# Dealing the first half's indexer tiles among product pairs, gating state-space output in SBUF halves, and exponentiating decay rows that are already on chip

## The chip, the cores and the metric

The kernel runs on one core of a Trainium2 chip. TensorE (PE) multiplies matrices from SBUF into eight PSUM banks; VectorE (DVE), ScalarE (ACT) and GpSimd (POOL) do the elementwise work; every transfer between the chip's memory and SBUF is issued on the queue of SyncE (SP). Each engine works through its own list of instructions in order, and waits at an instruction until what it needs is there. The metric is the device time of one execution in microseconds (us).

## The reference

One layer of a streaming encoder over 1024 positions of width 2048. One input projection makes every part:

```python
u = jnp.einsum('bsd,de->bse', h, w_in[layer])
q, k, v, z_attn, q_idx, k_idx, w_idx, z_ssd, xbc, dt_raw = _split_cols(u, IN_WIDTHS)
o_attn = _dsa_attention(q, k, v, q_idx, k_idx, w_idx) * jax.nn.silu(z_attn)
o_ssd = _ssd_mixer(xbc, z_ssd, dt_raw, conv_w[layer], conv_b[layer], dt_bias[layer], a_log[layer], d_skip[layer], ssd_norm_w[layer])
sub = jnp.einsum('bse,ed->bsd', jnp.concatenate([o_attn, o_ssd], axis=-1), w_out[layer])
h = _layer_norm(DEEPNORM_ALPHA * h + sub, ln_g[layer], ln_b[layer])
```

The attention has an indexer: 16 small heads give scores `relu(q_idx . k_idx)`, summed with the weights `w_idx`; each query keeps its top 256 admissible keys (by chunks of 64) and attends to those. The state-space mixer (SSD) makes, per group of four heads, decay matrices out of cumulative sums `a_cum`, a part within a chunk and a part from the state carried over, which is scaled by `exp(a_cum)`. Its output y is gated: `g = y * silu(z)`, divided by the root of the mean square over the group, times `norm_w`. All of it is float32.

## The kernel before, in words

**Float32 on the array.** Each matrix operand is split into a high and a low part (`xh`, `xl` of the activations, `wh`, `wl` of the weights) and a product is three matmuls: xh by wh, xl by wh, xh by wl. The splits are made by ACT (the high part) and DVE (the low part).

**Who sets the order.** Every step of the computation is a generator, a task with a priority, that says before each step what it needs: engines, free buffers, events (`Need`). `Flow` (line 353) keeps a clock for each engine by a model; whenever PE has been given one piece of the main stream, `pump` (line 476) takes tasks that `ready` (line 431) lets through, and their instructions are written behind those already there. So the order on all engines is fixed when the kernel is built, and each engine's list is one interleaving of main stream and tasks. All instructions are recorded at one helper line, L312, so the trace is read by the names of buffers: `pj` are the four PSUM banks of projections and products, `a` the three of scores and small products, `o` one more; `u` the 29 general SBUF buffers of 128x512, `s` larger ones, `xr`, `xh`, `xl` activations, `wr`, `wh`, `wl` weights; names such as `mx`, `my`, `y`, `zs`, `arow`, `ts`, `c` are arrays in the chip's memory.

**The main stream.** `units` (line 589) makes it out of `PLAN` (line 55). The positions are in two halves, h=1 the second and h=0 the first. First come nine tiles for h=1: `misc` (the indexer's key, its weights, and dt) and eight tiles `qi` of 128 indexer columns, that is, two indexer heads each. Then the same nine for h=0, with the `qi` tiles on 256 columns only (`s0=256`), because the first 256 positions keep all admissible keys. Then two groups of pairs of tiles. The two halves of the positions and the two tiles of a pair make a 2x2 block product that is computed with fewer block products out of sums of blocks, in four phases (`product`, line 663); within a phase, pairs are taken in couples of two. Group 0 has eight pairs (four couples): k, v, the q heads and the first xbc columns. Group 1 has xbc, zs and z. Last come seven output products on sums of blocks of the mixed output (`PRODUCTS`, line 67: A11, S3, S1, S2, A22, S4, A12), numbered 0 to 6, each of eight banks of 24 matmuls, and the layer norm.

**A qi tile's tail.** When its 48 matmuls have filled a `pj` bank, `t_qi` (line 1452) applies the rope on DVE (a shuffle and three multiplies or adds), which also frees the bank for PE; then for each head and block of queries PE computes scores into an `a` bank, ACT applies the relu there, and DVE multiplies by the head's weight and adds to the sum in `s` (`t_score`, line 1494). `t_topk` (line 1518) then finds each query's threshold in 32 rounds between ACT and DVE.

**State-space part.** `t_ssd` (line 1928) is a task for each half h and group g, in two steps cp=0,1 of 256 positions. A step loads xy, B and C, loads the decay rows `ar` from `arow` (all 128 partitions get each head's row), and later loads the same rows again in another arrangement, `ea`, with four transfers, and exponentiates them. `ev_y` signals that both steps have been written to the array `y`. `t_gate` (line 2046) loads two tiles of y and (unless they are still in SBUF) two of silu(z), which `s_zs` (line 1909) saved in `zs`; it multiplies, squares, sums by PE, scales, and writes two of the sixteen arrays `mx` of a half. The forms of the output products (`t_form`, line 1011) read `mx` back: one load for A11, two with a difference for S3, three with two sums for S1 and S2.

## Time and profile before

| | |
|---|---|
| time, median of 3 runs | 1709.56 us (1708.21 to 1709.71) |
| the profiled execution's own time | 1706.55 us |
| its span, first to last instruction | 1704.4 us |
| mean granted TensorE clock | 0.982 |
| PE busy | 1631.9 us (96%), 7996 matmuls |
| DVE busy | 1328.9 us (78%) |
| ACT busy | 985.3 us (58%) |
| POOL busy | 174.2 us (10%) |
| moved by DMA | 426.55 MB |

By the trace the stages lie so, in us from the start of the span: tiles for h=1 to 125; tiles for h=0 to 254; phase 0 of group 0 to 358.5, its other phases to 622; group 1 to 1329.5; output product 0 from there to 1392, product 1 to 1451, product 2 to 1517, the other four to 1692; the rest of the layer norm to 1704.4.

How to read it: the busy time of PE is the time in which some matmul was under way, and a matmul under a throttled clock is busy for longer, so a busy PE can still lose time. The granted clock stands beside it. A row of the view by windows gives the window, its length, then busy time and number of instructions of PE, of the weight loads, of DVE, ACT and POOL, then the granted clock, the busy share of the DMA engines and GB/s. A row of a timeline gives start, duration, engine, operation, and in brackets the idle time before it with what ended it.

### The profile page before, as it was taken

How to read it: one execution, taken by the hardware profiler on the slowest of the kernel's cores; microseconds unless marked ns; L12 is line 12 of the kernel's file. 1: busy time of each engine (PE TensorE's matmuls, PEld its weight loads, DVE VectorE, ACT ScalarE, POOL GpSimd, SP SyncE). 2: the span in 40 equal slices, each digit the busy share in tenths (PEclk: the TensorE clock that was granted, in tenths of full speed). 3: DMA queues.
4: the chain of work that ended last, by engine and by line, in shares of the span. 5: the costliest groups of instructions: out<-in, count | busy, mean ns of one | idle time of the engine just before them, and what ended most of it. 6: DMA issues, size and time to landing. Idle time of an engine off the chain costs nothing.

```text
span 1704.4 us, 24034 instructions
## 1 busy us (share of the span) xinstructions
PE 1631.9 (96%) x7996; PEld 1347.0 (79%) x7996; DVE 1328.9 (78%) x2411; ACT 985.3 (58%) x1750; POOL 174.2 (10%) x198
## 2 busy tenths in 40 slices
PE   9998889989998999999999999999999989899997
PEld 7787667868876878888888888888888768688885
DVE  5799989688878976767787678976687675649998
ACT  4554567988887568847444446785746443432330
POOL 0000000000000000212011201211111000000110
PEclk9998999999999999999999999999999999899999
DMA  8297523699978877568785487667989889767754
GB/s 302 70 313 275 207 99 120 225 353 329 351 261 304 305 267 259 194 218 297 273 313 190 162 281 232 204 198 226 316 309 332 288 292 301 251 240 266 242 191 155
DMA packets 203876, 426.55 MB, mean 250 GB/s; under 512 B 21224, under 2 KB 61288, under 8 KB 203752
## 3 DMA queue, kind: packets, MB, share of 16 engines
q1 hardware_dynamic: 203320, 424.63, 72.4%
q8 instruction: 63, 1.03, 0.2%
q14 instruction: 61, 0.50, 0.1%
q10 hardware_dynamic: 432, 0.39, 0.1%
HBM read 317.06 MB, written 107.87 MB: 249 GB/s over the span
## 4 chain that ended last, share of the span: by engine, by line
PE 53%; DVE 19%; ACT 11%; DMA 10%; issue 5%; SPq 1%; POOL 1%; DVEq 0%; ACTq 0%
PE pj L312 39%; PE a L312 11%; DVE u L312 8%; ACT u L312 5%; DVE wl L312 3%; DVE s L312 3%; PE o L312 3%; ACT wh L312 2%; DVE wr L312 2%; DMA wr<-wt 2%; DVE xl L312 1%; SPq L312 1%; DMA s<-xt 1%; DMA u<-xt 1%; DMA u<-o 1%
## 5 line engine op out<-in xcount | busy, mean ns | idle before, releaser
L312 PE MATMUL pj<-xh,wh 128*128 128x512 f32 (+1 forms) x1496 | 587.8, 393 | 27.1 <-DVE u L312 20.1
L312 PE MATMUL pj<-xl,wh 128*128 128x512 f32 (+1 forms) x1496 | 574.0, 384 | 1.2 <-DVE xl L312 1.1
L312 PE MATMUL pj<-xh,wl 128*128 128x512 f32 (+1 forms) x1496 | 574.0, 384 | 0.5 <-DVE wl L312 0.5
L312 DVE TENSOR_TENSOR wl<-wr,wh 128x1024 fp32r<-128x1024 f32 (+2 forms) x232 | 278.0, 1202 | 183.8 <-ACT wh L312 176.9
L312 ACT ACTIVATE wh<-wr 128x1024 fp32r<-128x1024 f32 (+2 forms) x242 | 248.4, 1031 | 189.8 <-PE pj L312 153.6
L312 PEld LDWEIGHTS pj<-xh,wh 128*128 128x128 f32 x1496 | 284.9, 190 | 83.3 <-issue 24.6
L312 PEld LDWEIGHTS pj<-xh,wl 128*128 128x128 f32 x1496 | 284.5, 190 | 56.3 <-DVE wl L312 1.0
L312 PEld LDWEIGHTS pj<-xl,wh 128*128 128x128 f32 x1496 | 285.3, 191 | 52.0 <-DVE xl L312 2.2
L312 PE MATMUL a<-u,u 128*128 128x512 f32 (+3 forms) x736 | 173.7, 357 | 7.7 <-DVE s L312 4.1
L312 DVE TENSOR_TENSOR u<-u,u 128x512 f32<-128x512 f32 (+6 forms) x231 | 149.7, 660 | 10.5 <-DMA u<-o 4.2
L312 PEld LDWEIGHTS a<-u,u 128*128 128x128 f32 x736 | 121.2, 191 | 44.6 <-DVE s L312 21.2
L312 PE MATMUL pj<-wh,xh 128*128 128x512 f32 x310 | 126.7, 409 | 15.3 <-ACT xh L312 8.2
L312 ACT ACTIVATE u<-a 128x512 fp32r<-128x512 f32 (+4 forms) x112 | 53.4, 489 | 137.8 <-DVE u L312 58.5
L312 ACT ACTIVATE u<-s,sm 128x768 bf16<-128x768 int16 (+7 forms) x132 | 129.5, 981 | 1.5
L312 ACT ACTIVATE u<-u 128x512 f32<-128x512 f32 (+4 forms) x165 | 91.0, 563 | 63.8 <-DVE u L312 55.7
L312 PE MATMUL pj<-wh,xl 128*128 128x512 f32 x310 | 122.3, 395 | 2.3 <-DVE xl L312 2.3
L312 PE MATMUL pj<-wl,xh 128*128 128x512 f32 x310 | 122.3, 394 | 0.0
L312 ACT ACTIVATE a<-a 128x512 f32<-128x512 f32 (+3 forms) x160 | 76.2, 503 | 65.8 <-PE a L312 64.4
L312 DVE TENSOR_TENSOR wr<-wr,wr 128x1024 f32<-128x1024 f32 (+1 forms) x87 | 106.1, 1220 | 7.7 <-DMA wr<-wt 7.3
L312 DVE TENSOR_TENSOR u<-pj,u 128x512 f32<-128x512 f32 (+2 forms) x112 | 74.5, 667 | 25.8 <-PE pj L312 23.9
L312 POOL TENSOR_SCALAR s<-s,sm 128x640 f32<-128x640 f32 (+7 forms) x64 | 60.1, 953 | 245.9 <-DVE sm L312 188.6
L312 PEld LDWEIGHTS pj<-wh,xh 128*128 128x128 f32 x310 | 59.0, 190 | 30.7 <-ACT xh L312 9.1
(254 smaller groups left out, 2151.2 us busy)
## 6 DMA issues: line engine op xcount, KB each, us to landing
wr<-wt SPq DMA_DIRECT2D x187, 512.0 KB, 5.1
u<-u SPq DMA_DIRECT2D x110, 256.0 KB, 4.8
wr<-t SPq DMA_DIRECT2D x44, 512.0 KB, 8.5
u<-wo SPq DMA_DIRECT2D x64, 256.0 KB, 6.1
ts<-u SPq DMA_DIRECT2D x64, 256.0 KB, 4.2
wr<-ts SPq DMA_DIRECT2D x32, 512.0 KB, 4.6
u<-mx SPq DMA_DIRECT2D x54, 256.0 KB, 6.3
s<-xt SPq DMA_DIRECT2D x24, 512.0 KB, 7.8
```

Of the source, the lines that this page charges most:

```text
L312: f(*args, **kw)
```

## The change

Three edits.

1. **Tiles of the first half.** The line of `PLAN` for h=0 goes. Its nine tiles (written by the same `plain`) are dealt among the four couples of group 0, phase 0: misc, couple 0, couple 1, qi a to d, couple 2, qi e to h, couple 3. The tiles read the x blocks that phase 0 reads anyway.
2. **Gating.** The arrays `y`, `zs` and the upper eight of `mx` (now pairs, `my`) are laid out so that both 128-row tiles of a group are one transfer of 128x2x256, half the positions. When silu(z) has been saved by the end of a step of `t_ssd`, the step's output stays in SBUF and goes straight to a `t_gate` for that step; only zz, the half of silu(z), is loaded. Otherwise y is saved and loaded as before, in halves. `t_gate` handles 256 positions at a time, except where silu(z) itself is still in SBUF (`wide`).
3. **Decay exponentials.** `ea` is computed by ACT out of the rows `ar` that are on chip, 64 partitions at a time, before `ar` is overwritten; the four transfers, the wait for a buffer between, and the one exponential on all 128 partitions go. Its buffer is asked for at the start of a step (`u=8 - cp`).

```diff
 PLAN = [
     (1, FIRST + QI[2:], 3),
-    (0, [("misc", 0)] + QI, 3),
     [(("k", 0), ("k", 1)), (("v", 0), ("v", 1))] + [(("q", n), ("q", n + 4)) for n in range(4)]
     + [(("xbc", (0, 2 * j)), ("xbc", (0, 2 * j + 1))) for j in range(2)],
     [(("xbc", (1, j)), ("xbc", (3, j))) for j in range(4)] + [(("xbc", (2, j)), ("xbc", (2, 2 + j))) for j in range(2)]
     + [(("zs", (n // 2, n % 2)), ("z", n)) for n in range(8)],
 ]
 GROUPS = [x for x in PLAN if isinstance(x, list)]
+OPENING = "m01abcd2efgh3"
...
             for ph in range(4):
-                for couple in couples:
+                for couple in [int(k) if k.isdigit() else k for k in OPENING] if (gi, ph) == (0, 0) else couples:
+                    if isinstance(couple, str):
+                        tile = ("misc", 0) if couple == "m" else QI["abcdefgh".index(couple)]
+                        for u in range(2):
+                            plain(0, tile, u, base)
+                        continue
+                    couple = couples[couple] if isinstance(couple, int) else couple
                     for f in range(1 + (ph < 3)):
                         for c in couple:
                             i = put(self.product(gi, c, pairs[c], ph, f, base + 2 * ph + f))
...
-        self.mixed = [[self.scratch(f"mx{h}_{e}", [P, HALF]) for e in range(16)] for h in range(2)]
+        self.mixed2 = [[self.scratch(f"my{h}_{g}", [2, P, HALF]) for g in range(4)] for h in range(2)]
+        self.mixed = [[self.scratch(f"mx{h}_{e}", [P, HALF]) for e in range(8)] + [m[j] for m in self.mixed2[h] for j in range(2)]
...
-        if self.ev_y[h, g].t is None:
-            yield Need()
-            fl.dma(self.zs_sc[h, g, j], x)
+        yield Need()
+        other = self.zg.get((h, g, 1 - j))
+        if other[0] is None if other else len(self.ydone[h, g]) < 2:
+            fl.dma(self.zs_sc[h, g][j], x)
             fl.free(x)
             x = None
         fl.signal(e)
         self.zg[h, g, j] = (x, e)
-        if (h, g, 1 - j) in self.zg:
-            fl.add(self.t_gate(h, g), 2, f"gate{h}{g}")
+        if other:
+            if x is not None:
+                fl.add(self.t_gate(h, g, (0, 1)), 2, f"gate{h}{g}")
+            else:
+                for cp in self.ydone[h, g]:
+                    fl.add(self.t_gate(h, g, (cp,)), 2, f"gate{h}{g}")
+
...
-            yield Need("", s4=1, u=7 - cp, keep=SKEEP)
+            yield Need("", s4=1, u=8 - cp, keep=SKEEP)
...
-            bn, xdt, xdd, hs = [fl.new("u", [P, 2, 256]) for _ in range(4)]
+            bn, xdt, xdd, hs, ea = [fl.new("u", [P, 2, 256]) for _ in range(5)]
+            ea = ea.rearrange("p a (b l) -> p a b l", b=2)
             rows = self.arow[h].rearrange("(c n) l -> c n l", c=4)[2 * cp:2 * cp + 2, 4 * g:4 * g + 4, :]
-            pairs = rows.rearrange("c (j q) l -> q c j l", q=2)
             for k in range(2):
                 fl.dma(ar[:, k], rows[k].partition_broadcast(P))
...
+            for q in range(2):
+                rq = slice(64 * q, 64 * q + 64)
+                fl.act(ea[rq], ar[rq].rearrange("p k (j q) l -> p k j q l", q=2)[:, :, :, q], AF.Exp)
...
-            yield Need("", u=1)
-            ea = fl.new("u", [P, 2, 2, P])
-            for q in range(2):
-                for k in range(2):
-                    fl.dma(ea[64 * q:64 * q + 64, k], pairs[q, k].partition_broadcast(64))
             yield Need("A")
             fl.act(ar, ar, AF.Exp, scale=-1.0)
-            fl.act(ea, ea, AF.Exp)
             yield Need("VG")
...
+            zz, landed = None, 0.0
+            if self.zg_there(h, g) and fl.avail("us"):
+                zz = fl.new("us", [P, 2, 256])
+                fl.dma(zz, self.zs_sc[h, g][:, :, cp * 256:cp * 256 + 256].rearrange("j p s -> p j s"))
+                landed = fl.cells[-1][0]
...
+            if self.zg_there(h, g):
+                fl.add(self.t_gate(h, g, (cp,), xy, zz), 2, f"gate{h}{g}", max(fl.clk["V"], fl.clk["G"], landed))
+                continue
             yield Need()
-            fl.dma(self.y_sc[h, g][:, :, cp * 256:cp * 256 + 256], xy)
+            self.ydone[h, g].append(cp)
+            fl.dma(self.y_sc[h, g][:, :, cp * 256:cp * 256 + 256].rearrange("j p s -> p j s"), xy)
             fl.free(xy)
+            fl.signal(self.ev_y[h, g, cp])
+            if self.zg_there(h, g):
+                fl.add(self.t_gate(h, g, (cp,)), 2, f"gate{h}{g}")
         fl.free(hs)
-        fl.signal(self.ev_y[h, g])
...
-    def t_gate(self, h, g):
+
...
+        w = 256 * len(cps)
+        cols = slice(256 * cps[0], 256 * cps[0] + w)
+        held = [self.zg[h, g, j] for j in range(2)]
+        wide = held[0][0] is not None
+        evs = () if xy is not None else tuple(self.ev_y[h, g, cp] for cp in cps)
+        yield Need("", us=(xy is None) * (1 if w == 256 else 2) + (zz is None and not wide), ev=evs + tuple(e for _, e in held))
...
+            if zz is None:
+                zz = fl.new("us", [P, 2, 256])
+                fl.dma(zz, self.zs_sc[h, g][:, :, cols].rearrange("j p s -> p j s"))
+            if xy is None:
+                xy = fl.new("us", [P, 2, 256])
+                fl.dma(xy, self.y_sc[h, g][:, :, cols].rearrange("j p s -> p j s"))
+            xs, zs, tiles = [xy], [zz], [xy, zz]
+            part = lambda t, j: t[0][:, j]
...
+        n = self.gated[h, g] = self.gated.get((h, g), 0) + len(cps)
+        if wide:
+            for j in range(2):
+                fl.dma(self.mixed[h][8 + 2 * g + j], xs[j])
+        else:
+            fl.dma(self.mixed2[h][g][:, :, cols].rearrange("j p s -> p j s"), xy)
+        if n == 2:
+            for j in range(2):
+                fl.signal(self.ev_mix[h, 8 + 2 * g + j])
+        fl.free(*tiles)
```

In the order, PE's rows go from 7392 to 7405, DVE's from 2279 to 2294, POOL's from 184 to 188, and ACT's keep their number; single transfers on SP go from 1315 to 1235: 64 of `arow` fewer, 14 fewer writes and 14 fewer reads of `y`, and 6 more writes and 6 more reads of `z`, the gates of the attention, which are saved when they are ready ahead of the attention's output.

**First place: PE at the end of the h=0 misc tile**, where the second of the h=0 tiles' banks follows it. A matmul row names the bank, the activation part, the weight part and the shape. Before, the misc tile and the first qi tile (`pj_1544`) are interleaved and the next qi tile, `pj_1609`, follows:

```order
L312 MATMUL pj_1544<-xh_1364,wl_1407 128x256
L312 MATMUL pj_1544<-xh_1368,wh_1406 128x256
L312 MATMUL pj_1544<-xl_1369,wh_1406 128x256
L312 MATMUL pj_1544<-xh_1368,wl_1407 128x256
L312 MATMUL pj_1609<-xh_1240,wh_1486 128x256
L312 MATMUL pj_1609<-xl_1241,wh_1486 128x256
L312 MATMUL pj_1609<-xh_1240,wl_1487 128x256
L312 MATMUL pj_1609<-xh_1244,wh_1486 128x256
```

With the change, the first of the two products of couple 0, `pj_1578`, follows the misc tile (`pj_1474`):

```order
L312 MATMUL pj_1474<-xh_1462,wl_1391 128x512
L312 MATMUL pj_1474<-xh_1466,wh_1390 128x512
L312 MATMUL pj_1474<-xl_1467,wh_1390 128x512
L312 MATMUL pj_1474<-xh_1466,wl_1391 128x512
L312 MATMUL pj_1578<-xh_1224,wh_1470 128x512
L312 MATMUL pj_1578<-xl_1225,wh_1470 128x512
L312 MATMUL pj_1578<-xh_1224,wl_1471 128x512
L312 MATMUL pj_1578<-xh_1228,wh_1470 128x512
```

What moved: tiles of 256 columns with a tail of scores no longer follow each other; a product on 512 columns stands there, and qi a comes after four such products.

**Second place: DVE ahead of the rope that frees a bank.** Before, `pj_1609` above takes the bank of `pj_1151`, the last but one qi tile of h=1; its rope is the shuffle and the three operations on `pj_1151` and `u_1595`:

```order
L312 TENSOR_TENSOR wl_1539<-wr_1202,wh_1538 128x1024
L312 SCALAR_TENSOR_TENSOR s_109_761<-a_1551,wsc_244,s_109_761 128x384
L312 SCALAR_TENSOR_TENSOR s_110_762<-a_1565,wsc_244,s_110_762 128x512
L312 TENSOR_TENSOR s_271_1532<-s_270_1530,s_271_1532 128x1024
L312 TENSOR_TENSOR s_270_1530<-xr_1534,s_270_1530 128x1024
L312 TENSOR_TENSOR wl_1587<-wr_1274,wh_1586 128x1024
L312 TENSOR_TENSOR u_1113<-u_1113,u_1393 128x512
L312 TENSOR_TENSOR u_1111<-u_1111,u_1113 128x512
L312 STREAM_SHUFFLE u_1595<-pj_1151 128x512
L312 TENSOR_TENSOR pj_1151<-pj_1151,u_642 128x512
L312 TENSOR_TENSOR u_1595<-u_1595,u_643 128x512
L312 TENSOR_TENSOR u_1594<-pj_1151,u_1595 128x512
```

With the change the same tile is `pj_1135`, and its bank goes to `pj_1632`, the second product of couple 0:

```order
L312 TENSOR_TENSOR s_271_1516<-s_270_1514,s_271_1516 128x1024
L312 TENSOR_TENSOR s_270_1514<-xr_1518,s_270_1514 128x1024
L312 TENSOR_TENSOR u_1097<-u_1097,u_1377 128x512
L312 TENSOR_TENSOR u_1095<-u_1095,u_1097 128x512
L312 TENSOR_TENSOR u_1541<-u_1082,u_1541 128x512
L312 TENSOR_TENSOR wl_1575<-wr_1258,wh_1574 128x1024
L312 STREAM_SHUFFLE u_1586<-pj_1135 128x512
L312 TENSOR_TENSOR pj_1135<-pj_1135,u_626 128x512
L312 TENSOR_TENSOR u_1586<-u_1586,u_627 128x512
L312 TENSOR_TENSOR u_1585<-pj_1135,u_1586 128x512
```

What moved: DVE's list there is nearly the same, with one more small operation ahead of the rope; PE's list has changed ahead of the bank's next use, which now follows the first 24 matmuls of `pj_1578`.

**Third place: SP in output product 2** (before) and the same forms' loads with the change. Before, forms of S1 (`xh_14456`, `xl_14458`, `u_14460` and the three from `mx_7`, `mx_15`) stand among a y write, four decay transfers, silu loads and y loads of the last SSD step, whose gated result goes to `mx_14` and `mx_15`:

```order
L312 DMA xh_14456<-mx_6_261 128x512
L312 DMA xl_14458<-mx_14_269 128x512
L312 DMA u_14460<-mx_6_277 128x512
L312 DMA y_1_326<-xh_13949 256x1x256
L312 DMA u_14503<-mx_7_262 128x512
L312 DMA u_14505<-mx_15_270 128x512
L312 DMA u_14507<-mx_7_278 128x512
L312 DMA u_14516<-arow_292 64x2x128 x4
L312 DMA s_5_400<-u_14430 128x512
L312 DMA xh_14528<-zs_1_0_339 128x512
L312 DMA u_14530<-zs_1_1_340 128x512
L312 DMA u_14532<-y_1_326 128x512
```

With the change, the loads of the same two forms read `my_3` (with `mx_6`, `mx_7`); the rest is weights (`wr`), one half of silu(z), one write of a gated half (`my_3_262`, which is of the other half of the positions), and two writes of forms to `s_5` and `s_6`:

```order
L312 DMA u_14314<-mx_6_269 128x512
L312 DMA u_14316<-my_3_258 128x512
L312 DMA u_14318<-mx_6_277 128x512
L312 DMA my_3_262<-u_13500 128x2x256
L312 DMA u_14341<-zs_1_326 128x2x256
L312 DMA s_5_384<-u_14239 128x512
L312 DMA xl_14391<-mx_7_270 128x512
L312 DMA u_14393<-my_3_258 128x512
L312 DMA u_14395<-mx_7_278 128x512
L312 DMA wr_14415<-ts_01_356 128x1024
L312 DMA xl_14423<-zs_2_327 128x2x256
```

What moved: the decay transfers and the y transfers are gone from between the loads and what follows them.

More of the change, by code (lines that the diff above doesn't have):

```diff
@@ L1924, in s_zs, with zg_there @@
         self.zg[h, g, j] = (x, e)
-        if (h, g, 1 - j) in self.zg:
-            fl.add(self.t_gate(h, g), 2, f"gate{h}{g}")
+        if other:
[4 more added lines that the diff above has]
+                    fl.add(self.t_gate(h, g, (cp,)), 2, f"gate{h}{g}")
+    def zg_there(self, h, g):
+        return all((h, g, j) in self.zg for j in range(2)) and self.zg[h, g, 0][0] is None
     def t_ssd(self, h, g):
@@ L2058, in t_gate @@
         yield Need("G")
-        for j in range(2):
-            fl.two(xs[j], xs[j], zg[j], ALU.mult)
+        for x, z in zip(xs, zs):
+            fl.two(x, x, z, ALU.mult)
         yield Need("A")
-        for j in range(2):
-            fl.act(zg[j], xs[j], AF.Square)
+        for x, z in zip(xs, zs):
+            fl.act(z, x, AF.Square)
         yield Need("G")
-        fl.two(zg[0], zg[0], zg[1], ALU.add)
+        fl.two(part(zs, 0), part(zs, 0), part(zs, 1), ALU.add)
         yield Need("P", a=1, sm=1)
```

46 lines of the change are left out of this document (21 added, 25 removed).

## The prediction

> **What bounds the kernel now.** I read the page first, then the view by windows along the stages.
>
> ```profile
> PE 1631.9 (96%) x7996; PEld 1347.0 (79%) x7996; DVE 1328.9 (78%) x2411; ACT 985.3 (58%) x1750; POOL 174.2 (10%) x198
> ...
> PEclk9998999999999999999999999999999999899999
> ```
>
> ```profile
> 24.00:125.00 101.00, 98.64 (x455) 80.83 (x456) 81.19 (x140) 52.52 (x97) 6.00 (x5) 1.00 0.59 206
> 125.00:254.00 129.00, 110.23 (x604) 89.47 (x603) 120.80 (x192) 73.58 (x127) 6.52 (x5) 0.91 0.54 197
> 254.00:358.50 104.50, 103.72 (x464) 84.82 (x463) 81.62 (x193) 88.32 (x176) 8.61 (x14) 1.00 0.59 214
> 358.50:622.00 263.50, 248.81 (x1075) 202.29 (x1074) 217.69 (x449) 200.50 (x377) 9.80 (x13) 0.98 0.88 312
> 622.00:1329.50 707.50, 703.62 (x3693) 591.66 (x3692) 532.69 (x983) 429.94 (x753) 115.37 (x130) 1.00 0.74 249
> 1329.50:1517.00 187.50, 169.23 (x858) 138.83 (x857) 114.41 (x188) 81.05 (x144) 8.91 (x7) 0.95 0.79 266
> 1517.00:1704.40 187.40, 175.38 (x770) 143.68 (x768) 167.66 (x250) 45.42 (x55) 17.41 (x12) 0.98 0.67 227
> ```
>
> PE is the bound, but not evenly. In group 1 (622 to 1329.5) it is busy for 703.6 of 707.5 us at a full clock: nothing is to be had there. It is idle for 18.8 us in the first half's tiles (125 to 254), for 14.7 in the rest of group 0 and for 18.3 in output products 0 to 2, and in the first and the last of these the clock is low too. In 125 to 254 it is DVE that is full, 120.8 of 129, while on either side of it DVE has some 20 us to spare. The view of waits says who is waited for, over the span and then in 125 to 254:
>
> ```profile
> PE pj L312 <- DVE u L312: 27.1, 6, 7.6
> PE pj L312 <- ACT xh L312: 8.9, 4, 4.5
> ```
>
> ```profile
> PE pj L312 <- DVE u L312: 15.6, 4, 7.6
> ```
>
> **What a stall in the tiles looks like**, in the timelines of PE and of DVE:
>
> ```profile
> 131.82 0.28 PE L312 MATMUL pj<-xh,wh 128*128 128x256 f32 x1
> ...
> 142.88 0.55 PE L312 MATMUL pj<-xh,wh 128*128 128x256 f32 x1 [7.59 <-DVE u L312]
> 143.24 0.41 PE L312 MATMUL pj<-xl,wh 128*128 128x256 f32 x1
> 143.45 0.41 PE L312 MATMUL pj<-xh,wl 128*128 128x256 f32 x1
> ```
>
> ```profile
> 135.18 1.22 DVE L312 TENSOR_TENSOR s<-s,s 128x1024 f32<-128x1024 f32 x1
> ...
> 140.05 0.72 DVE L312 STREAM_SHUFFLE u<-pj 128x512 f32<-128x512 f32 x1
> ...
> 142.05 0.69 DVE L312 TENSOR_TENSOR u<-pj,u 128x512 f32<-128x512 f32 x1
> ```
>
> ```profile
> 135.00:143.00 8.00, 0.41 (x4) 0.23 (x2) 7.83 (x12) 1.28 (x2) 0.00 (x0) 0.67 0.76 258
> 143.00:150.00 7.00, 7.00 (x34) 6.69 (x35) 6.79 (x11) 2.29 (x5) 1.04 (x2) 0.65 0.99 322
> ```
>
> DVE works without a gap (7.83 of 8 us), the rope that frees the bank ends at 142.7, and PE starts then. Its next matmuls come 0.21 us apart instead of 0.12, at a clock of 0.65 for 7 us. So a stall costs its length and then some.
>
> **What is lost in 125 to 254.** The groups of PE in that window:
>
> ```profile
> L312 PE MATMUL a<-u,u 128*128 128x512 f32 x136 | 45.0, 445 | 3.1 <-DVE s L312 2.1
> L312 PE MATMUL pj<-xh,wh 128*128 128x256 f32 x128 | 39.3, 307 | 15.7 <-DVE u L312 15.6
> L312 PE MATMUL pj<-xl,wh 128*128 128x256 f32 x127 | 38.1, 300 | 0.0
> L312 PE MATMUL pj<-xh,wl 128*128 128x256 f32 x127 | 37.9, 299 | 0.0
> L312 PE MATMUL pj<-xh,wh 128*128 128x512 f32 x16 | 6.4, 401 | 0.0
> ```
>
> The durations overlap, so I go by pitch. Where PE runs without a gap and at full clock, four output products of 192 matmuls each take 175 us, 228 ns for one of 512 columns:
>
> ```profile
> 1517.00:1692.00 175.00, 174.82 (x769) 143.54 (x768) 159.19 (x236) 45.42 (x55) 16.43 (x11) 1.00 0.68 231
> ```
>
> One of 256 columns takes 119 (the rows at 131.7 to 131.9). 382 by 119 is 45.5; 136 and three times 16 by 228 is 41.9; the 38 smaller ones, by their widths, are 5.0. That is 92.4 us of work in 129: **36.6 are lost**, 18.8 idle and 17.8 in a slow clock.
>
> **Edit 1, the tiles dealt out.** PE's work stays the same; its 604 matmuls and the 464 of phase 0 are mixed. DVE's work for both stretches is one row:
>
> ```profile
> 125.00:358.50 233.50, 213.94 (x1065) 174.29 (x1064) 202.42 (x384) 161.91 (x303) 15.13 (x19) 0.95 0.57 204
> ```
>
> PE alone would need 233.5 − 36.6 = 197, DVE alone 202.4: the two are nearly equal, so DVE need not hold PE up for long anywhere, but it has next to nothing in hand. The least gain is where DVE keeps the share that it reached in the tiles (120.8 of 129, 0.936): 202.4/0.936 = 216, a gain of 17. The most is all 36.6. I take **−26**, half way: DVE is then at 202.4 of 207.5, as full as in the 8 us of its row at 135. The first stall shows how close it is: counted in the order with these pitches, PE has 8.0 us more work ahead of `pj_1632` than it had ahead of `pj_1609`, so it asks for the bank at 143, and the rope, with one small operation more ahead of it, ends at about 143.3: the stall of 7.6 goes, with nothing in hand. The loads go past SP in another order; the DMA share of 0.54 to 0.59 in both stretches leaves room for them.
>
> **The rest of group 0.** Where phase 1 begins, PE has 15.8 us of 21.5 while DVE and ACT are full, the tail of the top-k rounds and scores:
>
> ```profile
> 358.50:380.00 21.50, 15.82 (x61) 11.97 (x60) 19.64 (x33) 16.79 (x31) 0.88 (x1) 0.92 0.90 325
> ```
>
> Idle there is 5.7 of the stage's 14.7 us. With couple 3 behind the last qi tile, some of that tail lies earlier under products; against that, scores that end later push top-k into phases 1 to 3. Between 0 and 14.7 I take those **−5**.
>
> **Edits 2 and 3 in output products 0 to 2.** The chain of waits there ends on transfers:
>
> ```profile
> 1389.33 6.51 DMA xh<-mx
> ...
> 1421.58 1.02 PE o L312 x16
> ...
> 1433.11 0.89 PE a L312 x8
> ...
> 1448.22 3.48 DMA u<-y
> ...
> 1468.80 2.27 DMA u<-arow
> ```
>
> ```profile
> 1392.00:1401.00 9.00, 2.05 (x9) 1.43 (x8) 7.61 (x12) 5.05 (x9) 1.77 (x1) 0.79 0.76 277
> ...
> 1467.00:1478.00 11.00, 4.24 (x18) 2.87 (x18) 9.05 (x14) 3.29 (x5) 0.00 (x0) 0.74 0.85 270
> ```
>
> Work in 1329.5 to 1517: three products of 192 by 228 ns are 131.3; the other 282 are 64 of 64 ns (the row of 16) and 218 of 111 (the row of 8), 28.3. That is 159.6 of 187.5: **28 lost**, 18.3 idle and 10 by the clock. The idle stands before banks whose forms come late, because the last SSD steps and their gating, with loads of decay rows and y, run among the forms in the same queues. In the order of before, PE's next bank stands behind ten or more instructions of other engines at three places here (product 0's eighth bank's operand, product 1's first, product 2's sixth); in the changed order at none, nor at the three places that it had in the tiles. Two SSD steps fewer are left for this stage (six for eight), and each has no y trip and no second load of its rows. Bounds: nothing, and all 28; what could make it worse is a form that reads a `my` half just written, which the order shows for none of S3's. I take **−23**, and leave 5 for forms of product 2 that stand close to their use.
>
> What edits 2 and 3 add elsewhere:
>
> ```profile
> L312 DVE SCALAR_TENSOR_TENSOR u<-u,dn,a 128x512 f32<-128x512 f32 x6 | 4.2, 739 | 0.0
> L312 DVE SCALAR_TENSOR_TENSOR u<-u,dn,o 128x256 f32<-128x256 f32 x20 | 8.6, 473 | 1.3 <-PE o L312 1.3
> ```
>
> ```profile
> L312 ACT ACTIVATE u<-u 128x512 f32<-128x512 f32 x66 | 41.0, 627 | 30.3 <-DVE u L312 26.9 <-DMA u<-arow 3.1
> ```
>
> ```profile
> L312 SPq DMA_DIRECT2D u<-arow x60: 573/604/922, 657.9 to 1468.8; - x60
> ```
>
> Gating in halves: four operations of 473 for two of 739, 0.4 us per group, and about as much for its small ones, under 8 us of DVE over eight groups. The exponential on 64 partitions twice costs at most 627 ns more, 10 us of ACT over 16 steps; and the buffer for it is held from the step's start. All that lies under PE in group 1, where DVE is at 533 and ACT at 430 of 707: **0**, and at most those 8 if the cover were gone. Off SP's list go 64 issues of 0.6 us, 39 us, which nothing but the stage above waits for.
>
> **The sum.** −26 − 5 − 23 = −54 against the profiled execution's 1706.55: 1652.5. The median lies 3.0 above that execution, so **1655 us**.
>
> [...]
>
> **The rivals.**
>
> *All stalls go.* −36.6, −14.7 and −28: −79, **1630**. For it: the order has no long block left. Against: DVE's 202.4 for PE's 197. Chance 0.10.
>
> *Part of the slow clock stays.* The row at 143 loses 2.4 us of 7 behind 7.6 us of idle, a third; by that share the 37.1 us of idle of both stages explain 12 of the 27.8 that the clock lost, and if the other 16 have another cause, they stay: −38, **1671**. For it: in that row the clock stays at 0.65 though PE has no gap. Against: in group 1, without stalls, it is 1.00 over 707 us. Chance 0.08.
>
> *Form waits return.* With tile tails pushed later, the forms of S1 stand right ahead of their use, and product 1 and 2 keep what they lose (three waits of 4 to 7 us and their clock, 18 in all): −36, **1673**. For it: the chain's load took 6.5 us from `mx`. Against: fewer transfers in the queue. Chance 0.12.
>
> *Slower.* The first half's scores end later, so its top-k and its attention do; six attention gates more go out to `z` and come back. Its last mixed block is written, counted in PE's work in the order, some 70 us later than before and 40 ahead of its use in product 1's operand. If ACT and DVE run behind that count by more than 40 us, every us is a stall at product 1; by 40 + 54 the gain is spent, and at 98 behind it is **1713**. Against: ACT is at 430 of 707 us in group 1. Chance 0.05.
>
> *Not what it says.* Were the silu halves not there when a step ends, y would still go through memory, and half of the 23 would stay, 1667; but the order shows two writes of y where there were 16. Chance 0.02.
>
> **How the numbers follow.** The forecast has the rest, 0.63, and by the bounds of its terms 1640 to 1666. The range takes in the cases at 1667, 1671 and 1673 with some room for their sizes, and stops short of the first rival: **1636 to 1684**, with 0.85 inside. What this kernel's measurement can tell from no change is about 0.2%, 3.4 us. Faster 0.92: all the cases but the slower one, less 0.03 for what may end at no change; same 0.03, slower 0.05.
>
> **What would show it.** The tiles and phase 0 end near 332 instead of 358.5, with DVE over 95% busy, no PE wait of over 4 us and a clock of 0.97 or more; the first output product starts near 1298; products 0 to 2 take about 164 us; group 1 keeps its 707. I am wrong if PE's waits for the rope persist between qi a to d and e to h (four tails stand together), or if product 1 waits for `mx`.

## The result, and the profile after

The changed kernel takes 1690.18 us (median of four runs, 1686.08 to 1696.48) where the kernel before, run beside it, takes 1709.26: a ratio of 0.9889, 95% interval 0.9859 to 0.9920. It is faster by 19 us. I had forecast 54, and 1690 lies outside the range of 1636 to 1684. The profiled execution is the slowest of the four, 1696.48, so the traces differ by 10.1 us, and the other 9 us of the gain stand in no trace. Each trace is one execution, and those of the changed kernel spread over 10 us, so that a few us of a stage's difference can be chance.

The page of the changed kernel, PE and the granted clock:

```profile
PE 1624.7 (96%) x7996; PEld 1341.5 (79%) x7996; DVE 1329.2 (78%) x2439; ACT 996.6 (59%) x1766; POOL 175.8 (10%) x205
...
PEclk9999999999998999999999999999999999999999
```

To compare stages I cut both traces at the first matmul of each stage: h=0 tiles with phase 0, the rest of group 0, group 1, output products 0, 1 and 2. (By this cut group 1 begins at 597 before; the prediction had put it at 622.) The view by windows of the kernel before, columns as in the prediction:

```profile
125.10:358.80 233.70, 214.15 (x1066) 174.42 (x1065) 202.32 (x384) 162.21 (x305) 15.13 (x19) 0.95 0.57 204
358.80:597.40 238.60, 225.71 (x977) 184.33 (x976) 202.98 (x424) 183.88 (x350) 9.26 (x12) 0.98 0.87 310
597.40:1329.70 732.30, 726.62 (x3791) 609.55 (x3790) 547.41 (x1008) 446.28 (x780) 115.90 (x132) 1.00 0.75 252
1329.70:1392.20 62.50, 58.33 (x303) 47.69 (x302) 37.36 (x66) 26.59 (x48) 2.70 (x2) 0.97 0.87 289
1392.20:1451.00 58.80, 51.85 (x255) 42.50 (x254) 35.37 (x56) 24.62 (x46) 3.06 (x2) 0.94 0.91 299
1451.00:1517.10 66.10, 58.95 (x302) 48.54 (x301) 41.68 (x67) 29.83 (x50) 3.15 (x3) 0.92 0.61 214
```

and of the changed kernel:

```profile
125.20:339.80 214.60, 206.53 (x1065) 169.42 (x1064) 198.59 (x336) 138.96 (x243) 20.19 (x18) 0.99 0.73 248
339.80:587.50 247.70, 226.56 (x973) 183.34 (x972) 192.81 (x417) 183.94 (x360) 14.39 (x15) 0.97 0.86 305
587.50:1323.00 735.50, 719.31 (x3706) 603.21 (x3705) 545.97 (x1038) 464.52 (x804) 97.86 (x126) 1.00 0.69 232
1323.00:1380.80 57.80, 53.87 (x271) 44.35 (x271) 42.26 (x77) 32.69 (x65) 3.06 (x3) 1.00 0.94 312
1380.80:1439.70 58.90, 58.47 (x327) 48.83 (x325) 37.89 (x72) 32.25 (x63) 8.33 (x8) 1.00 0.88 298
1439.70:1506.70 67.00, 62.90 (x346) 51.76 (x344) 49.17 (x91) 32.74 (x60) 6.27 (x5) 0.95 0.56 190
```

Since small matmuls move from stage to stage, I compare what each stage loses: its length less PE's work in it (matmuls of 512 columns at 227 ns, 384 at 174, 256 at 119, 128 at 109 to 112, the pitches of gap-free stretches). Two small kinds stand at nothing in it: 256 matmuls of the state-space steps on 64 columns of the array (64 ns each by the prediction's row of 16) and 64 matmuls of one column (some 110). They are about 23 us of PE work in every order, all of it in group 1 and the output products, so the losses of these stages are too high by that, here and in the table of the experiments.

| lost, us | before | changed | difference | forecast |
|---|---|---|---|---|
| h=0 tiles and phase 0 of group 0 | 40.1 | 21.1 | −19.0 | −26 |
| rest of group 0 | 19.1 | 28.5 | +9.4 | −5 |
| group 1 | 36.6 | 45.1 | +8.5 | 0 |
| output products 0 to 2 | 39.6 | 30.5 | −9.1 | −23 |
| sum | 135.4 | 125.2 | −10.2 | −54 |

With the two small kinds counted, group 1 loses 34 us instead of 23 and the products 19 instead of 30, where the prediction had 28 for them; the sum of both is 53 before and after. The first half's tiles did most of what they were to do. Behind them the program as a whole gained nothing: two stages lose 18 us more, one loses 9 less.

**Where group 0 loses.** The waits of ACT from 339.8 to 597, before and then changed (us in total, times, longest):

```profile
ACT u L312 <- DVE sm L312: 14.5, 11, 3.3
```

```profile
ACT u L312 <- DVE sm L312: 33.4, 16, 5.7
```

`sm` holds the thresholds of top-k, which go round between ACT and DVE. Timeline of ACT before, the first and the last of the 32 rounds of the first half's smaller block (128x384):

```profile
312.72 0.61 ACT L312 ACTIVATE u<-u,sm 128x384 bf16<-128x384 int16 x1
...
525.43 0.62 ACT L312 ACTIVATE u<-u,sm 128x384 bf16<-128x384 f32 x1 [0.38 <-DVE sm L312]
```

and of the changed kernel, with the next to last as well:

```profile
363.02 0.60 ACT L312 ACTIVATE u<-u,sm 128x384 bf16<-128x384 int16 x1
...
572.46 0.62 ACT L312 ACTIVATE u<-u,sm 128x384 bf16<-128x384 f32 x1 [5.67 <-DVE sm L312]
...
575.81 0.60 ACT L312 ACTIVATE u<-u,sm 128x384 bf16<-128x384 f32 x1
```

These rounds end 50 us later, though PE is 19 us earlier here. The rounds of the second half begin when they did (281 to 310 before, 286 to 294 changed), and end later too: blocks 4 and 5 at 647 instead of 582, blocks 6 and 7 at 763 instead of 703. The scores of the first half, which stood ahead of group 0, now share phase 0 with them and come first in priority.

What ACT waits does not say what PE loses. PE's longest waits in this stage (358.8 to 597.4 before, 339.8 to 587.5 changed), before and then changed:

```profile
PE pj L312 <- DVE u L312: 4.5, 1, 4.5
PE pj L312 <- ACT u L312: 3.4, 1, 3.4
```

```profile
PE pj L312 <- DVE u L312: 9.1, 4, 3.2
PE pj L312 <- ACT u L312: 8.8, 2, 8.6
```

The longest PE wait of the changed kernel is the 8.6 among them, in the timelines of PE and of ACT:

```profile
535.38 0.76 PE L312 MATMUL pj<-xh,wh 128*128 128x512 f32 x1 [8.56 <-ACT u L312]
```

```profile
527.39 2.43 ACT L312 ACTIVATE xh<-xr 128x512 fp32r<-128x512 f32 x4 [4.69 <-DMA xr<-xt]
...
533.20 0.92 ACT L312 ACTIVATE u<-s,sm 128x768 bf16<-128x768 f32 x1
...
534.12 1.13 ACT L312 ACTIVATE u<-s,sm 128x1024 bf16<-128x1024 int16 x1
535.15 0.19 ACT L312 ACTIVATION_READ_ACCUMULATOR u<-s,sm 128x1 f32 x1
```

ACT stands 4.7 us at the split of a reloaded x block whose transfer is late; what PE waits for stands behind it on ACT. The wait ends with the last of these rows: behind the splits come two rounds of top-k, which are 2.1 of the 8.6 us. The wait is no accident of this execution: at this place of the main stream (in the last quarter of the stage) PE waits 3.5 to 4.6 us in the seven orders of this document without edit 1, 6.1 to 8.8 in eight of the ten with it, and 4.0 and 5.1 in the other two. That the later top-k makes this stage lose 9 us is not shown.

**Where the state-space steps went.** Transfers of decay rows, two for each of 16 steps, from the first output product on: before

```profile
L312 SPq DMA_DIRECT2D s<-arow x9: 332/437/1482, 1329.3 to 1439.0; - x9
```

and changed

```profile
L312 SPq DMA_DIRECT2D s<-arow x14: 332/332/650, 1325.0 to 1467.0; - x14
```

Seven steps are left for the output products where there were four (one of the nine transfers belongs to a step begun ahead). I had counted six for eight.

### The profile page after: what moved, and what is told of

It reads as the page before. It is cut to its first block, busy times and chain, and to the rows that moved or that the text cites. A ratio compares the mean times of both kernels' runs of the same rounds, so it can differ in the third digit from the quotient of the medians.

```text
span 1694.7 us, 24018 instructions
## 1 busy us (share of the span) xinstructions
PE 1624.7 (96%) x7996; PEld 1341.5 (79%) x7996; DVE 1329.2 (78%) x2439; ACT 996.6 (59%) x1766; POOL 175.8 (10%) x205
## 4 chain that ended last, share of the span: by engine, by line
PE 49%; DVE 22%; ACT 12%; DMA 10%; issue 6%; SPq 1%; POOL 1%; DVEq 0%; ACTq 0%; POOLq 0%
PE pj L312 36%; PE a L312 11%; DVE u L312 9%; ACT u L312 6%; DVE wl L312 4%; DVE s L312 4%; PE o L312 3%; DMA wr<-wt 3%; ACT wh L312 2%; DMA u<-u 2%; DVE xl L312 2%; ACT s L312 2%; DVE wr L312 1%; ACT L312 1%; DMA u<-wo 1%
## 5 line engine op out<-in xcount | busy, mean ns | idle before, releaser
L312 DVE TENSOR_TENSOR u<-u,u 128x512 f32<-128x512 f32 (+6 forms) x206 | 131.6, 648 | 18.7 <-DMA u<-wo 10.6
L312 ACT ACTIVATE u<-s,sm 128x768 bf16<-128x768 int16 (+7 forms) x132 | 129.5, 981 | 15.2 <-DVE sm L312 13.7
L312 ACT ACTIVATE u<-u 128x512 f32<-128x512 f32 (+4 forms) x147 | 80.6, 558 | 62.1 <-DVE u L312 53.2
L312 DVE SCALAR_TENSOR_TENSOR u<-cv,cw,u 128x512 f32<-128x512 f32 x96 | 72.1, 757 | 9.3 <-ACT u L312 4.3
```

Of the source, the lines that this page charges most:

```text
L312: f(*args, **kw)
```

## Experiments

All times are medians, beside runs of the kernel before on the same chip. The table has what each order loses by stage, in the profiled execution, and the lead in us of the last write of the first half's attention output ahead of the start of product 1 (A), and of its state-space output ahead of product 2 (S); a negative lead is a write after the product began.

| kernel | edits | time | ratio, interval | tiles, phase 0 | rest of group 0 | group 1 | p0 | p1 | p2 | A | S |
|---|---|---|---|---|---|---|---|---|---|---|---|
| before | | 1709 | | 40.1 | 19.1 | 36.6 | 11.9 | 11.5 | 16.2 | 139 | 75 |
| changed | 1 2 3 | 1690.2 | 0.989 (0.986–0.992) | 21.1 | 28.5 | 45.1 | 8.9 | 7.2 | 14.4 | 53 | 23 |
| open_only | 1 | 1721.4 | 1.007 (1.006–1.009) | 20.3 | 23.8 | 36.4 | 6.7 | 20.2 | 43.7 | 39 | −44 |
| gate_ea | 2 3 | 1702.0 | 0.997 (0.995–0.999) | 38.0 | 19.9 | 41.6 | 6.9 | 6.9 | 16.0 | 128 | 25 |
| gate_only | 2 | 1715.1 | 1.003 (1.001–1.004) | 38.1 | 19.0 | 59.7 | 5.7 | 5.0 | 16.7 | 137 | 55 |
| ea_only | 3 | 1708.5 | 0.999 (0.998–1.000) | 38.0 | 18.6 | 43.4 | 10.9 | 9.3 | 15.3 | 134 | 40 |
| open_ea | 1 3 | 1708.7 | 1.000 (0.999–1.001) | 20.9 | 26.7 | 48.6 | 9.6 | 6.7 | 28.3 | 120 | −21 |
| before_m280 | margin 280 | 1738.9 | 1.017 (1.015–1.019) | 44.6 | 27.2 | 72.9 | 6.2 | 4.6 | 15.6 | 151 | 88 |
| before_m320 | margin 320 | 1725.1 | 1.010 (1.008–1.011) | 36.0 | 20.9 | 54.7 | 15.5 | 5.9 | 19.4 | 139 | 47 |
| after_m280 | 1 2 3, margin 280 | 1714.4 | 1.003 (1.002–1.005) | 20.1 | 13.7 | 43.2 | 4.7 | 43.7 | 17.8 | −57 | −17 |
| deal_late2 | 1 2 3, dealt otherwise | 1704.9 | 0.998 (0.997–0.999) | 23.3 | 33.7 | 60.4 | 6.7 | 6.5 | 3.0 | 137 | 33 |
| deal_even | 1 2 3, dealt otherwise | 1692.0 | 0.991 (0.989–0.992) | 15.7 | 32.7 | 46.8 | 7.1 | 8.6 | 12.3 | 76 | 35 |
| deal_last1 | 1 2 3, dealt otherwise | 1693.8 | 0.990 (0.988–0.992) | 20.2 | 30.3 | 55.0 | 6.2 | 7.5 | 3.5 | 133 | 39 |
| buf7 | 1 2 3, 7 buffers | 1708.7 | 1.000 (0.998–1.002) | 20.2 | 23.3 | 52.3 | 10.6 | 31.3 | 3.2 | −29 | 58 |
| ssd_first | 1 2 3, priority | 1727.3 | 1.010 (1.008–1.012) | 20.8 | 24.6 | 46.9 | 34.0 | 30.3 | −0.1 | −41 | 138 |
| topk_first | 1 2 3, priority | 1692.8 | 0.990 (0.988–0.992) | 21.1 | 23.9 | 53.8 | 10.0 | 8.4 | 5.3 | 141 | 70 |
| gate_ea_tk0 | 2 3, priority | 1706.1 | 0.998 (0.997–0.999) | 38.3 | 30.6 | 52.0 | 8.6 | 5.9 | 1.3 | 135 | 116 |

### One edit at a time

Theory A put group 1's loss down to edit 1, theory B to edits 2 and 3. Edit 1 alone is the first two hunks of the diff (`PLAN`, `OPENING`, the loop over it); edit 3 alone is the two places shown here and the second loads of the rows that they replace, edit 2 alone the rest:

```diff
-            yield Need("", s4=1, u=7 - cp, keep=SKEEP)
+            yield Need("", s4=1, u=8 - cp, keep=SKEEP)
...
+            for q in range(2):
+                rq = slice(64 * q, 64 * q + 64)
+                fl.act(ea[rq], ar[rq].rearrange("p k (j q) l -> p k j q l", q=2)[:, :, :, q], AF.Exp)
```

> Edit 1 alone (the tiles dealt out; gating and decay rows as before). By the trace of the changed kernel, PE begins phase 1 of group 0 about 19 us earlier and loses 9 of them again until group 1. Theory A: what group 1 loses there (some 9 us more than before) comes from edit 1 too, because the first half's top-k and attention end later: then this kernel is at 1700 to 1709, and its group 1 shows PE waits for attention and top-k work that the kernel before does not have. Theory B: group 1's loss comes from edits 2 and 3: then group 1 here is as clean as before, and the kernel is at 1698 to 1701, with the output products' stalls (about 18 us idle) still there.

> Edits 2 and 3 without edit 1 (nine tiles of the first half in a row as before). Theory A (group 1's loss is edit 1's): group 1 stays clean, the output products gain 9 to 23 us, the kernel is at 1687 to 1701. Theory B (group 1's loss is made by the halves and by the exponential in the steps of the state-space part): group 1 loses some 9, the output products gain 9, and the kernel is at 1706 to 1712.

> Edit 2 alone. If gating from SBUF is what helps the output products, most of what edits 2 and 3 do together is here: within 4 us of the kernel with both. Rival: the decay rows' transfers were the wait there (2.3 us in the chain of waits, and 39 us of SP's issues over the program): then this one is within 3 us of 1709.

> Edit 3 alone. By theory a small effect, 1705 to 1710: one transfer wait of 2.3 us less in output product 2, and one buffer of 29 held longer in each step. Rival: the transfers were a good part of the stalls in the output products, or the buffer held delays the steps: then more than 5 us away from 1709, on either side.

Edit 1 alone is slower, by 12 us: beyond every time that I had given it. Its tiles gain the same 20 us as in the changed kernel, its group 1 loses what it lost before by the table (28 us for 23 with the small matmuls counted), and it loses 71 us in the output products. Product 2 of this kernel in the view by windows, the wait of its PE that is longest, and the transfers of decay rows from product 0 on:

```profile
1431.80:1533.30 101.50, 82.24 (x428) 68.09 (x428) 60.64 (x110) 44.02 (x87) 12.45 (x10) 0.83 0.66 207
```

```profile
1491.12 1.87 PE L312 MATMUL a<-o,u 128*128 128x1 f32 x8 [7.43 <-DVE u L312]
```

```profile
L312 SPq DMA_DIRECT2D u<-arow x36: 573/602/1017, 1325.0 to 1488.6; - x36
L312 SPq DMA_DIRECT2D s<-arow x16: 332/430/727, 1306.3 to 1471.8; - x16
```

Eight of sixteen steps are left for the output products, and the first half's last gated output is written 44 us after the product that reads it has begun. The wait shown is at a gate's small matmuls: PE has the step's own instructions in its list and stands at them.

Edits 2 and 3 without edit 1 gain 7 us, in the output products and, by 2, in the tiles, and group 1 loses 5 more. That is theory B's distribution at a smaller price, and its total (1706 to 1712) is wrong; theory A's (1687 to 1701) ends 1 us short of the time. Edit 2 alone is slower by 6 us (group 1 loses 23 more, the products 12 less), outside both ranges that I had given it. Edit 3 alone is no change, as expected. The effects do not add: +12, +6 and −1 alone make −19 together. So neither theory holds as I put it.

### The same work in another order

```diff
-    MARGIN = 300.0
+    MARGIN = 280.0
```

The constant says how long before PE's clock, by the planner's model, the inputs of a task that needs PE must be there for the task to count as ready. Theory R says that any new order draws its stalls anew, theory M that they follow from the edits.

> The kernel before with one constant of the planner 7% smaller (its margin ahead of PE's clock, 280 ns instead of 300): the same work, another order. In its order 10 of the 16 steps of the state-space part stand behind the start of the output products or close to it, where the kernel before has 6. Theory R (any change of the planner's order draws a new set of stalls in group 1 and in the output products, of several us either way): the tiles of the first half lose 38 to 40 us as before, and group 1 and the output products together differ from the 77 us that they lose before by more than 5 us; the time is off 1709 by more than 4. Theory M (losses follow from what the edits do): within 3 us of 1709, each stage within 3 us.

> The same constant 7% larger (320 ns). Theory R: off 1709 by more than 4 us, in a direction that the size of the constant does not tell; theory M: within 3 us of 1709.

> The changed kernel with the constant at 280. Theory R: phase 1 of group 0 still begins with about 20 us lost in the tiles and phase 0, and the rest differs from the changed kernel's 105 us lost behind it by more than 5 us. Theory M: within 5 us of 1690 and the same losses by stage within 3.

(The number of steps given for the first of these does not fit the order that ran: by its trace, 3 of the 16 steps load their decay rows behind the start of the output products, where the kernel before has 4.) Twenty ns of margin, with the same instructions, cost the kernel before 30 us one way and 16 the other, and the changed kernel 24. Two of these three are more than the whole change moves. All three are slower; whether the orders of the kernel before and of the changed one are lucky draws, three runs do not tell. The first half's tiles differ little (36 to 45, and 20.1 to 21.1 with edit 1); what varies is what comes behind. Group 1 of the kernel before with a margin of 280, and its longest PE wait there:

```profile
610.20:1382.90 772.70, 745.40 (x3849) 625.54 (x3848) 556.76 (x1043) 459.37 (x814) 116.02 (x133) 0.98 0.71 240
```

```profile
1059.37 0.79 PE L312 MATMUL pj<-xh,wh 128*128 128x512 f32 x1 [7.50 <-DVE u L312]
```

Group 1 loses 37 to 73 us over the seven orders without edit 1, and the kernel before is the lowest of them: the "703.6 of 707.5 busy" that I took for a property of the stage was one of the order.

In the changed kernel with a margin of 280, it is product 1 that loses 43.7 us. The window of product 1, its longest wait, the window behind that wait, and the chain that ended last from 1386.9 on:

```profile
1339.60:1453.90 114.30, 92.83 (x508) 75.07 (x509) 76.70 (x161) 52.23 (x115) 12.66 (x16) 0.90 0.77 255
```

```profile
1400.94 0.80 PE L312 MATMUL pj<-wh,xh 128*128 128x512 f32 x1 [9.45 <-ACT xh L312]
```

```profile
1400.90:1408.00 7.10, 6.72 (x17) 4.77 (x17) 4.01 (x8) 1.26 (x2) 0.00 (x0) 0.51 0.84 280
```

```profile
1386.90 7.49 DMA u<-o
...
1394.48 1.32 DVE u L312 x3
1395.80 5.34 DMA mx<-u
...
1401.59 6.49 DMA u<-mx
```

The wait of 9.45 us ends with ACT's split of a form whose last load from `mx` landed at 1398.4; eight operations of a state-space step (2.4 us) stand ahead of that split on ACT. The chain begins within this wait: an attention output is loaded, gated, written to `mx` at 1395.8 and read back at once for a form of the product that had begun at 1339.6, 21 us of transfers and arithmetic in a row. It reaches PE only at 1415.35, where PE, at half its clock from 1400.9 to 1408, waits 0.76 us more. This is the mechanism of my rival "Slower", and the lead of −57 us says the same; how much of the 43.7 us it makes is not shown.

### Did the decay transfers make edit 1 slow?

> Edits 1 and 3 without edit 2. Edit 1 alone was at 1721, with 71 us lost in the output products where five of eight late steps of the state-space part, each with its four decay transfers and its y trip, fall on product 2. If the decay transfers made that loss, it goes here: 1690 to 1700. If the trip of y through memory made it, it stays: 1712 to 1722. By theory R neither: the time lies anywhere between, and goes with how many of the steps are left for product 2 in this order (3, where edit 1 alone has 5 and the changed kernel 4): about 1700.

The kernel has the gating of the kernel before, none of the lines of edit 2. It is at 1708.7, 13 us under edit 1 alone, and at none of the three times that I had given. Product 2 still loses 28.3, with the state-space output written 21 us after its start, where it was 44. The loss goes with the lead (S), and removing transfers is one of the things that move it.

### Leads as the rule

Theory D: with the tiles dealt out, what decides is whether the first half's outputs are there when the products that read them begin. Four orders of the changed kernel, each from one of these edits (`deal_late2`, `deal_even`, `buf7`, `ssd_first`):

```diff
-OPENING = "m01abcd2efgh3"
+OPENING = "m01abcd2ef3gh"
...
-OPENING = "m01abcd2efgh3"
+OPENING = "m0ab1cd2ef3gh"
...
-            yield Need("", s4=1, u=8 - cp, keep=SKEEP)
+            yield Need("", s4=1, u=7 - cp, keep=SKEEP)
...
-            fl.add(self.t_ssd(h, g), 3 + h, f"ssd{h}{g}")
+            fl.add(self.t_ssd(h, g), 2.2 + 0.1 * h, f"ssd{h}{g}")
```

> The changed kernel with the tiles dealt misc, couples 0 and 1, qi a to d, couple 2, qi e and f, couple 3, qi g and h. Theory D (with the tiles dealt out, what decides is whether the first half's attention and state-space outputs are written before the products that read them, product 1 and product 2, begin): in this order PE's last instruction of the first half's attention stands 190 us of PE work ahead of product 1, and only 5 of 16 state-space steps are left for the output products. So product 1 and 2 lose no more than in the changed kernel (7 and 14 us), phase 1 begins with 20 to 26 lost as there, and the time is 1680 to 1695. Theory R alone (each order draws its stalls): the time is anywhere from 1690 to 1720.

> The changed kernel with two qi tiles after each couple. Here 10 state-space steps stand ahead of the output products, more than in the changed kernel, but the last attention instruction of the first half stands 16 us of PE work behind the start of product 1. Theory D: product 1 loses over 25 us, waiting for forms that read the attention's late outputs, and the time is 1705 to 1730. If only the number of late state-space steps counted, it would be 1680 to 1690.

> The changed kernel with a state-space step asking for 7 free buffers (as before the change) and not 8. Theory D: attention is done 160 us of PE work ahead of product 1, 7 steps are left for the output products: product 1 and 2 lose 5 to 20 each, the time is 1685 to 1705. Theory B2 (the eighth buffer is what delayed the steps): group 1 loses 8 us less than in the changed kernel, and the time is below 1684.

> The changed kernel with the state-space steps given a priority ahead of the attention. They get ahead (three groups are through by 840 us of PE work, where the changed kernel has two), and the first half's attention ends 11 us of PE work behind the start of product 1. Theory D: product 1 loses over 25 us, and the time is 1705 to 1730, though no instruction was added. Theory R alone: nothing ties the loss to product 1.

The places that these texts give for the attention and for the steps do not fit the orders that ran: by the traces the attention's last write stands ahead of product 1 by 137, 76, −29 and −41 us. It is late in `buf7`, for which I had given 160 ahead, and not late in `deal_even`, for which I had given 16 behind. So `buf7` (1708.7 for 1685 to 1705) and `deal_even` (1692.0 for 1705 to 1730) missed their ranges on a false lead, and only `deal_late2` and `ssd_first` test the theory by their expectation: the second is in its range, the first is not. As a rule across the table, found from these runs and not forecast, D stands. Product 1 loses 20 us or more at the four lowest leads A (39, −29, −41, −57: 20.2, 31.3, 30.3, 43.7) and 5 to 12 at 53 and more. Product 2 loses 28 to 44 at S of −21 and −44, and at most 19.4 at all others, 17.8 at −17 among them. But D does not give the time: `deal_late2` has both leads and 16 us in the three products, and takes 1704.9, because its group 1 loses 60. A priority that brings the state-space steps ahead of the attention costs 37 us without an instruction added; one buffer fewer to ask for costs 19, and group 1 loses 52, so theory B2 falls.

### Top-k first, and its control

Theory K: the later top-k rounds bring the late attention, this the late state-space steps, and those the lost gain.

```diff
-            fl.add(self.t_topk(h, blocks), 1 + (blocks[0] == 6) / 2, f"topk{h}")
+            fl.add(self.t_topk(h, blocks), -1 + (blocks[0] == 6) / 20, f"topk{h}")
```

> The changed kernel with the top-k rounds given a priority ahead of all other tasks; no instruction is added. Theory K (edit 1 pushes the top-k rounds of both halves 50 to 60 us later, the attention follows, and the state-space steps, which come last in priority, land in the output products): with top-k first, attention and state-space output are written 122 and 60 us of PE work ahead of products 1 and 2, where the changed kernel has 40 and 17. So the tiles and phase 0 lose 20 to 23 us as before, products 0 to 2 together lose 15 to 22 where the changed kernel loses 31, and the time is 1673 to 1688. Theory R alone: any order draws its stalls anew, the time is anywhere from 1690 to 1720.

> Edits 2 and 3 without edit 1, with the same priority for top-k: the control. Without edit 1 the attention was 113 us of PE work ahead of product 1 already, and is 117 here; the state-space output goes from 14 to 97 ahead of product 2. Theory K: the tiles and phase 0 lose 38, products 0 to 2 lose 15 to 22 where edits 2 and 3 alone lose 30: 1685 to 1698, some 15 us over the kernel with edit 1 and top-k first. If top-k first were what helps and edit 1 were not, both would be at the same time within 5 us.

> The changed kernel with the last qi tile behind couple 3 (misc, couples 0 and 1, a to d, couple 2, e to g, couple 3, h). In its order the attention stands 115 us of PE work ahead of product 1, the state-space output 31 ahead of product 2, and PE's next instruction stands behind ten or more instructions of other engines at two places only, one of them the beginning of phase 1 (30 instructions). By theory D product 1 loses under 9 us and product 2 under 16, group 1 loses 40 to 48, and the beginning of phase 1 costs 5 to 10 us more than in the changed kernel: 1683 to 1700.

(The third has `OPENING = "m01abcd2efg3h"`.) The order did as K said: blocks 4 to 7 end at 503 and 720 instead of 647 and 763, the first half's (which now come behind) at 639, and the attention leads product 1 by 141 us instead of 53. The products lose 23.7 instead of 30.5, a little over what I gave them. The time did not follow: 1692.8, no better than the changed kernel. Group 1, and product 2, of this kernel:

```profile
583.80:1331.30 747.50, 728.09 (x3756) 609.99 (x3754) 552.11 (x1043) 466.72 (x821) 92.02 (x124) 0.99 0.70 237
...
1453.70:1505.20 51.50, 49.12 (x241) 40.39 (x240) 30.10 (x47) 20.78 (x30) 5.88 (x4) 1.00 0.44 146
```

Product 2 has almost no loss left, and group 1 loses 53.8 where the changed kernel loses 45.1. The control without edit 1 shows the same trade: products 15.8 for 29.8, group 1 52.0 for 41.6, the rest of group 0 30.6 for 19.9. The control is at 1706, outside its range as well. `deal_last1` is in its range, with products 1 and 2 as the rule says and group 1 at 55 instead of 40 to 48. The sum of group 1 and the three products is 68 to 79 in nine of these orders (76 before, 76 changed, 71 `gate_ea`, 68 `gate_ea_tk0`, 78 `topk_first`, 72 `deal_last1`), and 87 to 111 in the others, among them every one with a late lead. Where small matmuls of attention and state-space steps leave the products, group 1 loses more; a few us of that are the unpriced work of these matmuls, and that the rest are the same waits in another place is not shown. Theory K holds for the leads and falls as the reason for the lost gain.

No order that I ran beats the changed kernel: `deal_even`, `topk_first` and `deal_last1` are at 1692 to 1694, within its own spread of 1686 to 1696.

## Why the prediction was wrong

**Edit 1: −26, measured −19.** The mechanism was right and the size off, at the place where I chose. In ten orders with edit 1, tiles and phase 0 lose 15.7 to 23.3 us, in seven without it 36 to 45; no other effect here is as steady. I had set 17 as the least gain, from DVE at its share of 0.936, and taken half way to all 36.6. DVE reached 198.6 of 214.6 us, 0.925, close to that share; but that DVE was the limit is not shown, for `deal_even` loses less with DVE at 0.896:

```profile
126.10:332.20 206.10, 200.65 (x1050) 165.14 (x1049) 184.65 (x325) 141.42 (x247) 12.82 (x16) 1.00 0.69 238
```

The term that was too large is the upper bound. I called 17.8 of the 36.6 us a slow clock, but by its row (0.91 over 129 us) the clock accounts for at most 11.6. In the changed kernel 8.1 us of the 21.1 are idle and some 2 are clock; in `deal_even` 5.5 of the 15.7 are idle and the clock is full. The 10 or 11 us that remain in both are busy time of PE at a full clock, beyond the pitches that I count with, and dealing the tiles out could not win them. What they are stays open. The stall of 7.6 us went as worked out, with nothing in hand: a wait of 1.5 us is left, up to 144.9.

**The clock.** The rival in which part of the slow clock stays has fallen as to the clock: in the tiles and phase 0 it is 0.99 instead of 0.95, with no wait over 2.9 us. (The row at 143, which I took as a clock that stays at 0.65, is a mean: in the timeline the matmuls stand 0.21 us apart for 5 us and at the full clock's pitch after that.) A full clock without longer waits agrees with the Trainium skill, "TensorE: Matmul & The Clock Gate", section "What's actually happening", which sets the window of idleness at some 3.4 us. The rival was right, though, that some of what I had booked as clock has another cause and stays: it is among the 10 us above.

**The rest of group 0: −5, measured +9.** The step that failed is that the tail of top-k would lie earlier under products. I named the opposite in the same sentence and gave it no price. Top-k of the first half begins 50 us later and ends 50 us later, and ACT waits for its thresholds 33 us instead of 14.5. PE is idle for 21 us of the stage instead of 13. Of these 8 us, 4 are one wait that edit 1 makes longer in most orders, 8.6 us instead of 4.5, begun by a late x block. With the second half's rounds brought forward (`topk_first`) that wait is 8.8 and the stage loses 23.9, so the later top-k is shown and its price is not. Over the seven orders that keep the tiles as in the changed kernel's string the stage loses 14 to 29 us, over those without edit 1 19 to 31; so the 9 us are the size in these two orders and not a constant of the edit.

**Group 1: 0, measured +8.5 (+11 with the small matmuls counted).** I took a stage that is busy for 99% as one that stays so. The order of group 1 is made anew by every edit ahead of it, and the runs with another margin show what this alone is worth: +18 and +36 us in the kernel before, −2 in the changed one. What makes one order's group 1 lose 37 and another's 73 stays open; I found waits at different places in each, and no cause common to them.

**The output products: −23, measured −9.** The step "two SSD steps fewer are left for this stage" was wrong: seven are left where there were four. And the order's lack of long blocks did not mean that the waits were gone; the changed kernel has its waits in smaller pieces, and product 2 keeps 14.4 of 16.2. With edits 2 and 3 alone it keeps 16.0: the loads of y and of decay rows stood in its chain, and taking them out won nothing there. Beneath that lies the assumption that a stall removed from a stage is removed from the program. Group 1 and the products together lose 76 us before and 76 after by the table, 53 and 53 with the small matmuls counted.

**The rivals.** "Slower" had the right mechanism at the right size of the shift: the first half's last mixed block is written at 1328 instead of 1253, 75 us later, and the lead went from 139 to 53 us without being used up. It decides in three other orders with edit 1 (`after_m280`, `buf7`, `ssd_first`), so its chance of 0.05 looks too small. "Form waits return" was nearest in its time, 1673: products 1 and 2 keep 21.6 of 27.7 us, as it says. That its total is only 17 us short rests on nothing else in it, for it has no loss in group 0 or group 1.

## What to carry to other kernels

Where a planner or a scheduler sets the order, first run the unchanged kernel with a meaningless change to it: here 20 ns of a margin were worth 16 to 30 us, and a forecast for an edit to this kernel has at least that width. Price a removed stall as moved, not as gone, until it is clear who takes its time: work of low priority comes later when PE comes earlier, and what reads its results has a deadline. Before busy time of an engine is booked as a slow clock, set it beside the granted clock of the window: what the clock does not account for may stay.

## What the runs showed of the hardware that I had not expected

Runs of one order spread more than the first runs of the kernel before let expect: those lie within 1.5 us, but 19 later ones from 1704.5 to 1715.3, and those of the changed kernel from 1686.1 to 1696.5. Those of `gate_ea` fall in two groups, seven from 1699.4 to 1702.1 and three from 1709.7 to 1711.1. With one program the order is the same each time, so what differs is when work and transfers end; waits on late transfers such as that of ACT at 527 are where I would look, but no run here shows it. And the slow clock behind a long wait was seen again: behind the 8.56 us of the changed kernel the first matmul took 0.76 us, where matmuls of this shape otherwise take 0.39.
